# Start addresses of the moving operand in a float32r encoder layer, and another order at its end

## The chip, the cores and the metric

The kernel runs on one core of a Trainium2 chip. The metric is the device time of one execution in microseconds. Three runs of the kernel before took 2140.52, 2140.80 and 2141.89 us; the median is 2140.8 us.

## The reference: what is computed

One inference step of one layer of a streaming encoder, for 256 prompt frames and 32 sample frames (288 together) of width 2048, all in float32:

```
x = x + 1/2 * swiglu(rmsnorm(x, norm_ffn1), w_ffn1_in, w_ffn1_out)      # 2048 -> 2 x 5504 -> 2048
h = rmsnorm(x, norm_mix) @ w_in                                         # columns split among three groups of heads
x = x + concat[GLA 1024 | differential attention 512 | memory attention 512] @ w_o
x = x + 1/2 * swiglu(rmsnorm(x, norm_ffn2), w_ffn2_in, w_ffn2_out)
y = rmsnorm(x, norm_final)
def rmsnorm(x, g): return x * rsqrt(mean(x * x) + 1e-6) * g
def swiglu(x, w_in, w_out):
    gate, up = split(x @ w_in, 2)
    return (silu(gate) * up) @ w_out
```

The memory attention reads 256 memory tokens, which have a projection of their own (`w_mem_kv`). Beside y the step returns keys, values and states.

## The kernel before, in words

**Layout.** The residual `x_res` is kept transposed: the 2048 features lie as 16 blocks of 128 partitions, and each block holds 288 columns, one for each frame. A weight matrix is the stationary operand of a product, in tiles of 128 x 128, and a block of activations of 128 x 288 is the moving operand.

**Split products.** A float32 value is written as the sum of two parts, "high" (rounded to float32r) and "low" (what is left), both of them float32r. Weights are split into `wh` and `wl`, activations into `uh` and `ul` (normed input), `hh` and `hl` (hidden activations), `cdh`/`cdl` and `gch`/`gcl` (outputs of the heads). Three products replace one: wh with high, wh with low, wl with high. `split` (L101) does the first on ScalarE and the second on VectorE.

**Weights.** `add_group` lists all weights in chunks of up to 512 KB in the order of use. `load_chunk` (L163) issues one DMA for each on SP's queue, `split_chunk` (L191) splits it. `consume` (L215) gives the next chunk to the products and on the way brings the splits three chunks ahead and the loads six chunks ahead.

**`gemm` (L271)** makes one output of two blocks of 128 features (`nblk` = 2) in one PSUM tile of two banks. For each chunk of up to four rows of blocks it issues, for block 0 and then block 1, the products of wh with high and low, and then in the same way those of wl with high. Between chunks, `side` gives small steps of other work (attention, transposes, statistics) a place in TensorE's order; each such step is a function in one of four queues (`Thread`), and `need(mark)` runs a queue until a marked step is done.

**Stages.** Memory projection (`mem_group`, products of 512 columns), first feed-forward (`ffn("a", ...)`), input projection of the heads (`MIX`), `w_o` in two halves of eight outputs, second feed-forward (`ffn("b", ..., final=True)`). A feed-forward handles its 43 hidden blocks in two halves of 22 and 21: `gemm` with `w_in` on the normed input, then eight outputs g of `gemm` with `w_out` on the hidden blocks; the second half has 21 rows of blocks in six chunks (4, 4, 4, 4, 4, 1).

**Where the blocks lie.** All blocks of `uh`, `ul`, `hh` and `hl` stand 320 elements (`NS`, 1280 bytes) apart, of which 288 (`NT`) are used, and their tiles begin at 32 modulo 256 bytes of a partition (`uh` at 21024, `ul` at 41504, `hh` at 152096, `hl` at 180256). So every block begins at 32 modulo 256. The operands of `w_o` stand 288 elements (1152 bytes) apart, in tiles that begin at 32 modulo 256 too (`cdh` at 188960, `gch` at 152096), so that blocks begin at 32 and 160 in turn. The tiles of `wh` and `wl`, and each 128-column block in them, begin at 32 modulo 256.

**The end.** After output g of the last half, `final_pair(g)` (L1286) multiplies the two blocks with the final gain into `xg`, adds their squares into `acc` (`prep_sq`) and puts a step on `t_main` that transposes them with TensorE and copies them into the six output tiles `Y`. After g = 6 a step `f7` sums `acc` over the partitions. For g = 7 both blocks get their residual add and their square one after the other; then (L1320 on) TensorE sums the squares for the three groups of frames `T3`, VectorE adds up, `rsq` computes the scale, `need("y7")` transposes the last pair, and the six output tiles are scaled on VectorE and ScalarE in turn and sent by SP.

Of the kernel before, what the change touches and what calls it, by code (L numbers as in the profile page):

```python
# [19 lines left out]
P = 128  # L20
NT = 288
NS = 320
D = 2048
KB = 16
NF = 43
# [15 lines left out]
def hybrid_step_kernel(  # L41
# [40 lines left out]
    def mm(out, lhsT, rhs, start=True, stop=True):  # L82
        pe.matmul(out, lhsT, rhs, start=start, stop=stop)  # L83
# [17 lines left out]
    def split(hi, lo, src):  # L101
        act.copy(hi, src)  # L102
        tt(lo, src, hi.bitcast(F32), ALU.subtract)
# [21 lines left out]
    def kparts(n):  # L125
        return [4] * (n // 4) + ([n % 4] if n % 4 else [])
# [133 lines left out]
    def side(most=2):  # L260
        for t in threads:
            if most and t.can():
                t.step()
                most -= 1
# [3 lines left out]
            t = next(t for t in threads if any(x[1] == mark for x in t.q))  # L268
            t.step()

    def gemm(nchunk, xs, nblk=2):  # L271

        ps = psm.tile([P, 2, 512], F32, tag="m", name=f"m{nxt[2]}")
        k = 0
        for ci in range(nchunk):
            nk, (wh, wl) = consume()
            for part in range(2):
                for b in range(nblk):
                    cs = slice(b * P, (b + 1) * P)
# [12 lines left out]

    fstack = [None]

# [54 lines left out]
    x_res = const.tile([P, KB, NT], F32, name="x_res")  # L349
    G = const.tile([P, G_N], F32, name="G")  # L350
    lam = const.tile([P, 1], F32, name="lam")
    uh = const.tile([P, KB, NS], F32R, name="uh")[:, :, :NT]
    ul = const.tile([P, KB, NS], F32R, name="ul")[:, :, :NT]
    acc = const.tile([P, NT], F32, name="acc")
    dkc = const.tile([P, 4, P], F32, name="dkc")
    dvc = const.tile([P, 512], F32, name="dvc")
# [1 line left out]
    Bs = const.tile([P, 160], F32, name="Bs")  # L358
    mkn = ft.tile([P, P], F32, name="mkn")
    gdk = const.tile([P, 64], F32, name="gdk")  # L360
    mats = const.tile([P, 442], F32, name="mats")
    bcols, tri, smask = mats[:, 0:2], mats[:, 2:130], mats[:, 130:418]

    def gcol(i):
        return G[:, i:i + 1]
# [18 lines left out]

    T3, SR = (0, 128, 160), slice(96, 128)

    def tok_sums(ps, block):

        for t, t0 in enumerate(T3):
            mm(ps[:, t:t + 1], block[:, t0:t0 + P], ones[:, 0:1])  # L390

    fresh = [True]

    def prep_sq(i):
# [9 lines left out]

    def prep_u(i, g0):
        for b in (2 * i, 2 * i + 1):
            gsplit(uh[:, b, :], ul[:, b, :], x_res[:, b, :], gcol(g0 + b))

    def later_R(name):

# [8 lines left out]


    hp = fstack[0][1]
    mTh = hp.tile([P, 22, NS], F32R, tag="hh", name="mTh").rearrange("p a t -> p (a t)")[:, :4096]
    mTl = hp.tile([P, 22, NS], F32R, tag="hl", name="mTl").rearrange("p a t -> p (a t)")[:, :4096]
    mTh = mTh.rearrange("p (k m) -> p k m", m=256)
    mTl = mTl.rearrange("p (k m) -> p k m", m=256)
    mss = sm("mss")
    mrs = sm("mrs")

# [265 lines left out]
    def ffn(tag, mark, g_next, final=False):  # L694
        hp, fp = fstack[0][1], fstack[0][2]

        def ft(nm, bufs):
            return fp.tile([P, 2, NT], F32, tag=nm, bufs=bufs, name=f"{nm}_{tag}")

        def u(k):  # L700
            return uh[:, k, :], ul[:, k, :]

        for half, (a, b) in enumerate(HALVES):
            hh = hp.tile([P, 22, NS], F32R, tag="hh", name=f"hh{tag}{half}")[:, :, :NT]
            hl = hp.tile([P, 22, NS], F32R, tag="hl", name=f"hl{tag}{half}")[:, :, :NT]
            f = a
            while f < b:
                pair = f + 1 < b
                n = 2 if pair else 1
                ps = gemm(4, u)  # L710
                need(mark)
                gs = ft("gs", 1)[:, :n]
                sg = ft("sg", 2)[:, :n]
                mul(gs, ps[:, :n, :NT], Rb(n))
                act.activation(gs, gs, AF.Silu)  # L715
                mul(sg, gs, Rb(n))
                if pair:
                    side()
                    ps = gemm(4, u)
                    up = ps[:, :2, :NT]  # L720
                else:
                    up = ps[:, 1:2, :NT]
                hm = ft("hm", 1)[:, :n]
                mul(hm, up, sg)
                split(hh[:, f - a:f - a + n, :], hl[:, f - a:f - a + n, :], hm)
                f += n
                if f == NF:
                    exp_tables()
                side()
            for g in range(8):  # L730
                ps = gemm(len(kparts(b - a)), lambda k: (hh[:, k, :], hl[:, k, :]))
                xs = x_res[:, 2 * g:2 * g + 2, :]
                if final and half == 1 and g == 7:
                    sq = sq2("sql")
                    last_sq.append(sq)
                    for j in range(2):
                        stt(xs[:, j, :], ps[:, j, :NT], 0.5, xs[:, j, :], ALU.mult, ALU.add)
                        act.activation(sq[:, j, :], xs[:, j, :], AF.Square)
                else:
                    stt(xs, ps[:, :, :NT], 0.5, xs, ALU.mult, ALU.add)  # L740
# [11 lines left out]


    mstack = ExitStack()
    t4p = mstack.enter_context(tc.tile_pool(name="t4p", bufs=8))
    mxp = mstack.enter_context(tc.tile_pool(name="mxp", bufs=1))
    tlp = mstack.enter_context(tc.tile_pool(name="tlp", bufs=2))
# [417 lines left out]
    later_R("mix")  # L1175

    def u(k):
        return uh[:, k, :], ul[:, k, :]

    for kind, c0, g in MIX:  # L1180
        if kind == "glr":
# [98 lines left out]

    later_R("ffn2")
    open_ffn()
    Y = {}
    last_sq = []

    def final_pair(g):  # L1286
        if not Y:
            for t in range(3):
                for hf in range(2):
                    Y[t, hf] = c4(f"y{t}{hf}")  # L1290
        xp = x_res[:, 2 * g:2 * g + 2, :]
        xg = fstack[0][2].tile([P, 2, NT], F32, tag="sg", bufs=2, name="xg")
        for b in range(2):
            ts(xg[:, b, :], xp[:, b, :], gcol(G_FIN + 2 * g + b))
        if g < 7:
            prep_sq(g)
        hf, c0 = divmod(g * 256, 1024)

        def f():
            ps = s1("yt")  # L1300
            for t in range(2):
                for b in range(2):
                    tr(ps[:, t * 256 + b * P:t * 256 + (b + 1) * P], xg[:, b, t * P:(t + 1) * P])
            for t in range(2):
                act.copy(Y[t, hf][:, c0:c0 + 256], ps[:, t * 256:(t + 1) * 256])
# [3 lines left out]
            act.copy(Y[2, hf][96:128, c0:c0 + 256], ps[96:128, :256])  # L1309
        t_main.add(f, f"y{g}", delay=2)  # L1310
        if g == 6:
            def f7():
                ps = s1("yss0")
                tok_sums(ps, acc)
                act.copy(yr[:, 4:7], ps[:, 0:3])
            t_main.add(f7)

    yr = sm("yr")
    ffn("b", "R_ffn2", None, final=True)
    ps = s1("yss")  # L1320
    for j in range(2):
        for t, t0 in enumerate(T3):
            mm(ps[:, 4 * j + t:4 * j + t + 1], last_sq[0][:, j, t0:t0 + P], ones[:, 0:1])
    tt(yr[:, 8:11], ps[:, 0:3], yr[:, 4:7], ALU.add)
    tt(yr[:, 8:11], ps[:, 4:7], yr[:, 8:11], ALU.add)
    rsq(yr[:, 0:3], yr[:, 8:11], float(D))
    need("y7")
    for k, (hf, t, parts) in enumerate(((0, 0, 2), (0, 1, 1), (0, 2, 1), (1, 2, 1), (1, 0, 1), (1, 1, 1))):
        rows = slice(0, P) if t < 2 else slice(96, P)
        dst = y_prompt[0, t * P:(t + 1) * P] if t < 2 else y_sample[0]  # L1330
        n = 1024 // parts
        for c in range(0, 1024, n):
            y = Y[t, hf][rows, c:c + n]
            if k % 2 == 0:
                ts(y, y, yr[rows, t:t + 1])
            else:
                gscale(y, y, yr[rows, t:t + 1])
            sp.dma_start(dst[:, hf * 1024 + c:hf * 1024 + c + n], y)
# [59 lines left out]
```

## Time and profile before

| what | value |
|---|---|
| median of three runs | 2140.8 us |
| the profiled execution | 2142.87 us |
| its span, first to last instruction | 2141.1 us |
| mean granted clock of TensorE | 0.997 |
| TensorE busy | 2125.7 us, 99% |
| VectorE busy | 1116.7 us, 52% |
| ScalarE busy | 867.2 us, 41% |
| DMA: moved, mean rate | 353.75 MB, 165 GB/s |

Busy times of TensorE overlap: the products are pipelined, and each is recorded with its way through the array. A product of 288 columns has about 294 ns in the profile, while the next one starts some 130 ns after it. So what counts for the time is the distance between starts, not the length of one. In the names of a row, "m<-uh,wh" means: a PSUM tile m is written from the moving operand uh and the weights wh.

### The profile page before, as it was taken

To read this page: it belongs to the slowest core of one execution; us is meant where nothing else is said; L and a number is where in the kernel's file an instruction comes from. 1 tells how busy PE (TensorE), PEld (TensorE's weight loads), DVE (VectorE), ACT (ScalarE), POOL (GpSimd) and SP (SyncE) were. 2 spreads that over 40 slices of the span, in tenths; PEclk is the share of its full clock that TensorE was granted. 3 is DMA by queue.
4 is the path that set the end of the run, shared out by engine and by line. 5 is a ranking of instruction groups with operands and counts; after the bars stand their busy time and mean duration, and the time that the engine had idled before them with its cause. 6 is when DMAs were issued, how large, how long until landed. Compare 5 with 4: busy or idle time off the path is not lost.

```text
span 2141.1 us, 37537 instructions
## 1 busy us (share of the span) xinstructions
PE 2125.7 (99%) x16014; PEld 2102.4 (98%) x16014; DVE 1116.7 (52%) x1318; ACT 867.2 (41%) x1112; POOL 4.6 (0%) x11
## 2 busy tenths in 40 slices
PE   9999999999999999999999999999999999999997
PEld 7999999999999999999999999999999999999997
DVE  6754544445454455554665666445544444445443
ACT  6643333333333344334544444333333333333443
POOL 0000000000000000000000000000000000000000
PEclk9999999999999999999999999999999999999999
DMA  7656555555555545555455345555555555555553
GB/s 253 182 178 199 170 169 179 164 164 173 169 159 168 175 158 158 180 144 147 121 157 152 123 158 165 172 167 167 160 170 168 166 165 174 170 167 159 163 160 117
DMA packets 351555, 353.75 MB, mean 165 GB/s; under 512 B 14112, under 2 KB 343324, under 8 KB 351388
## 3 DMA queue, kind: packets, MB, share of 16 engines
q1 hardware_dynamic: 351388, 351.36, 53.9%
q8 instruction: 125, 2.05, 0.4%
q14 instruction: 42, 0.34, 0.0%
HBM read 345.59 MB, written 5.64 MB: 164 GB/s over the span
## 4 chain that ended last, share of the span: by engine, by line
PE 97%; DVE 1%; ACT 1%; DMA 1%; issue 0%; SPq 0%; ACTq 0%; DVEq 0%
PE m L83 93%; DMA ws<-in_w_mem_kv_dram 1%; PE go L83 1%; PE mm L83 0%; DVE wl L90 0%; ACT wh L102 0%; PE mo L83 0%; DVE ul L99 0%; PE gK L83 0%; PE msc L83 0%; PE dsc L83 0%; PE do L83 0%; PE sums L83 0%; DVE acc L90 0%; PE yt L87 0%
## 5 line engine op out<-in xcount | busy, mean ns | idle before, releaser
L90 DVE TENSOR_TENSOR wl<-ws,wh 128x1024 fp32r<-128x1024 f32 (+2 forms) x665 | 781.2, 1189 | 665.9 <-ACT wh L102 636.3
L102 ACT CAST wh<-ws 128x1024 fp32r<-128x1024 f32 (+2 forms) x665 | 665.3, 1018 | 657.9 <-PE m L83 513.9
L83 PE MATMUL m<-uh,wh 128*128 128x288 f32 x3392 | 912.4, 296 | 0.0
L83 PE MATMUL m<-ul,wh 128*128 128x288 f32 x3392 | 907.0, 294 | 0.0
L83 PEld LDWEIGHTS m<-uh,wh 128*128 128x128 f32 x3392 | 637.2, 188 | 2.7 <-issue 1.8
L83 PEld LDWEIGHTS m<-ul,wh 128*128 128x128 f32 x3392 | 637.6, 188 | 0.3
L83 PE MATMUL m<-uh,wl 128*128 128x288 f32 x3392 | 515.5, 294 | 0.0
L83 PEld LDWEIGHTS m<-uh,wl 128*128 128x128 f32 x3392 | 470.6, 188 | 0.0
L83 PE MATMUL m<-hhb,wh 128*128 128x288 f32 x688 | 184.7, 295 | 0.0
L83 PE MATMUL m<-hha,wh 128*128 128x288 f32 x688 | 184.3, 295 | 0.0
L83 PE MATMUL m<-hlb,wh 128*128 128x288 f32 x688 | 184.1, 294 | 0.0
L83 PE MATMUL m<-hla,wh 128*128 128x288 f32 x688 | 184.0, 293 | 0.0
L83 PEld LDWEIGHTS m<-hlb,wh 128*128 128x128 f32 x688 | 129.1, 188 | 0.0
L83 PEld LDWEIGHTS m<-hla,wh 128*128 128x128 f32 x688 | 129.1, 188 | 0.0
L83 PEld LDWEIGHTS m<-hhb,wh 128*128 128x128 f32 x688 | 129.1, 188 | 0.0
L83 PEld LDWEIGHTS m<-hha,wh 128*128 128x128 f32 x688 | 129.0, 188 | 0.0
L83 PE MATMUL m<-hha,wl 128*128 128x288 f32 x688 | 106.3, 294 | 0.0
L83 PE MATMUL m<-hhb,wl 128*128 128x288 f32 x688 | 106.1, 294 | 0.0
L83 PEld LDWEIGHTS m<-hha,wl 128*128 128x128 f32 x688 | 96.0, 188 | 0.0
L83 PEld LDWEIGHTS m<-hhb,wl 128*128 128x128 f32 x688 | 95.9, 188 | 0.0
L715 ACT ACTIVATE gs_b<-gs_b 128x576 f32<-128x576 f32 (+1 forms) x22 | 14.8, 674 | 84.6 <-DVE gs_b L93 84.6
L102 ACT CAST hhb<-hm_b 128x576 fp32r<-128x576 f32 (+1 forms) x22 | 14.6, 662 | 83.2 <-DVE hm_b L93 83.2
(284 smaller groups left out, 1178.0 us busy)
## 6 DMA issues: line engine op xcount, KB each, us to landing
ws<-in_w_ffn_in_dram SPq DMA_DIRECT2D x336, 512.0 KB, 4.1
ws<-in_w_ffn_out_dram SPq DMA_DIRECT2D x160, 512.0 KB, 3.5
ws<-in_w_in_dram SPq DMA_DIRECT2D x80, 512.0 KB, 3.7
ws<-in_w_o_dram SPq DMA_DIRECT2D x32, 512.0 KB, 3.5
ws<-in_w_mem_kv_dram SPq DMA_DIRECT2D x15, 512.0 KB, 5.6
ws<-in_w_ffn_out_dram SPq DMA_DIRECT2D x16, 256.0 KB, 2.7
ws<-in_w_ffn_in_dram SPq DMA_DIRECT2D x16, 256.0 KB, 3.5
x<-in_x_prompt_dram SPq DMA_DIRECT2D x4, 512.0 KB, 7.2
```

What stands on the lines that cost most here:

```text
L83: pe.matmul(out, lhsT, rhs, start=start, stop=stop)
L90: dve.tensor_tensor(out, a, b, op=op)
L102: act.copy(hi, src)
L715: act.activation(gs, gs, AF.Silu)
```

## The change

All blocks of `uh`, `ul`, `hh` and `hl` are moved by 36 elements (`SH`, 144 bytes) inside their tiles, so that they begin at 176 modulo 256 bytes. `uh` and `ul` become one tile `uhl`, which is 8 elements longer than both together; `mats` is 8 elements shorter, so that all tiles behind them keep their place. The tiles of `hh` and `hl` get 64 elements more. The memory projection uses the same tiles, but not the shift. Ahead of the mixer's pools stands a tile of 16 elements (64 bytes), which moves all the mixer's tiles: the operands of `w_o` begin at 96 and 224 modulo 256 bytes in turn.

The last `gemm` (g = 7 of the last half) holds its last two chunks back (`last=2`): after four chunks as before, block 0 gets all its products of the last two (15), and then block 1 gets its own. `final_last` takes the place of what followed: residual add, square and gain for each block, sums of squares added in one PSUM tile `yss` (set to zero by a product with zeros in the step "yss", where the sums of `acc` are added too), transposes and copies for each block apart. The output tiles are scaled and sent in another order: the two of 32 rows come last.

```diff
+SH = 36
...
-    def gemm(nchunk, xs, nblk=2):
+    def gemm(nchunk, xs, nblk=2, last=0):
...
-        for ci in range(nchunk):
+        for ci in range(nchunk - last):
...
+        held = [consume() for _ in range(last)]
+        for b in range(nblk if last else 0):
+            cs = slice(b * P, (b + 1) * P)
+            o, k_ = ps[:, b, :NT], k
+            for i, (nk, (wh, wl)) in enumerate(held):
+                for j in range(nk):
+                    xh, xl = xs(k_ + j)
+                    mm(o, wh[:, j, cs], xh, False, False)
+                    mm(o, wh[:, j, cs], xl, False, False)
+                    mm(o, wl[:, j, cs], xh, False, i == last - 1 and j == nk - 1)
+                k_ += nk
         return ps
+
+    def blocks(pool_, n, name, pad=0, **kw):
+        t = pool_.tile([P, n * NS + pad], F32R, name=name, **kw)
+        return t, lambda k, m=1: (t[:, SH + k * NS:SH + k * NS + NT] if m == 1 else
+                                  t[:, SH + k * NS:SH + (k + m) * NS].rearrange("p (k t) -> p k t", t=NS)[:, :, :NT])
...
-    uh = const.tile([P, KB, NS], F32R, name="uh")[:, :, :NT]
-    ul = const.tile([P, KB, NS], F32R, name="ul")[:, :, :NT]
+    _, uhl = blocks(const, 2 * KB, "uhl", 8)
...
-    mats = const.tile([P, 442], F32, name="mats")
+    mats = const.tile([P, 434], F32, name="mats")
...
-            hh = hp.tile([P, 22, NS], F32R, tag="hh", name=f"hh{tag}{half}")[:, :, :NT]
-            hl = hp.tile([P, 22, NS], F32R, tag="hl", name=f"hl{tag}{half}")[:, :, :NT]
+            hh, hl = (blocks(hp, 22, f"h{c}{tag}{half}", 64, tag=f"h{c}")[1] for c in "hl")
...
+                end = final and half == 1 and g == 7
+                ps = gemm(len(kparts(b - a)), lambda k: (hh(k), hl(k)), last=2 if end else 0)
...
+                if end:
+                    final_last(ps, xs)
+                    continue
...
+    mstack.enter_context(tc.tile_pool(name="pad", bufs=1)).tile([P, 16], F32, name="pad")
...
+    def tok_squares(block, stop):
+        for t, t0 in enumerate(T3):
+            mm(yss[0][:, 0, t:t + 1], block[:, t0:t0 + P], ones[:, 0:1], False, stop and t == 2)
...
             def f7():
-                ps = s1("yss0")
-                tok_sums(ps, acc)
-                act.copy(yr[:, 4:7], ps[:, 0:3])
-            t_main.add(f7)
+                yss.append(s2("yss"))
+                dve.memset(zero3, 0.0)
+                mm(yss[0][:, 0, 0:3], ones, zero3, True, False)
+                tok_squares(acc, False)
+            t_main.add(f7, "yss")
+
+    def final_last(ps, xs):
+        need("yss")
+        xg, sq = gained(7), sq2("sql")
+        pt = []
+        for j in range(2):
+            stt(xs[:, j, :], ps[:, j, :NT], 0.5, xs[:, j, :], ALU.mult, ALU.add)
+            act.activation(sq[:, j, :], xs[:, j, :], AF.Square)
+            ts(xg[:, j, :], xs[:, j, :], gcol(G_FIN + 14 + j))
+        for j in range(2):
+            tok_squares(sq[:, j, :], j == 1)
+            pt.append(s1(f"yl{j}"))
+            if j == 0:
+                for t, t0 in enumerate(T3):
+                    tr(pt[0][:, t * P:(t + 1) * P], xg[:, 0, t0:t0 + P])
+
+        def keep(j):
+            c = 768 + j * P
+            for t in range(2):
+                act.copy(Y[t, 1][:, c:c + P], pt[j][:, t * P:(t + 1) * P])
+            act.copy(Y[2, 1][SR, c:c + P], pt[j][SR, 256:384])
+        for t, t0 in enumerate(T3):
+            tr(pt[1][:, t * P:(t + 1) * P], xg[:, 1, t0:t0 + P])
+        keep(0)
+        rsq(yr, yss[0][:, 0, 0:3], float(D))
+        keep(1)
...
-    for k, (hf, t, parts) in enumerate(((0, 0, 2), (0, 1, 1), (0, 2, 1), (1, 2, 1), (1, 0, 1), (1, 1, 1))):
+    for k, (hf, t, parts) in enumerate(((0, 0, 2), (0, 1, 1), (1, 0, 1), (1, 1, 1), (0, 2, 1), (1, 2, 1))):
```

More of the change, by code (lines that the diff above doesn't have):

```diff
@@ L385, in hybrid_step_kernel @@
     T3, SR = (0, 128, 160), slice(96, 128)
-    def tok_sums(ps, block):
-        for t, t0 in enumerate(T3):
-            mm(ps[:, t:t + 1], block[:, t0:t0 + P], ones[:, 0:1])
     fresh = [True]
@@ L406, in prep_u @@
         for b in (2 * i, 2 * i + 1):
-            gsplit(uh[:, b, :], ul[:, b, :], x_res[:, b, :], gcol(g0 + b))
+            gsplit(uhl(b), uhl(KB + b), x_res[:, b, :], gcol(g0 + b))
     def later_R(name):
@@ L421, in hybrid_step_kernel @@
     hp = fstack[0][1]
[L422 to L425, printed above, removed]
+    mTh, mTl = (blocks(hp, 22, f"mT{c}", 64, tag=f"h{c}")[0][:, :4096].rearrange("p (k m) -> p k m", m=256)
+                for c in "hl")
     mss = sm("mss")
@@ L700, in u @@
         def u(k):
-            return uh[:, k, :], ul[:, k, :]
+            return uhl(k), uhl(KB + k)
         for half, (a, b) in enumerate(HALVES):
-            hh = hp.tile([P, 22, NS], F32R, tag="hh", name=f"hh{tag}{half}")[:, :, :NT]
-            hl = hp.tile([P, 22, NS], F32R, tag="hl", name=f"hl{tag}{half}")[:, :, :NT]
+            hh, hl = (blocks(hp, 22, f"h{c}{tag}{half}", 64, tag=f"h{c}")[1] for c in "hl")
             f = a
@@ L724, in ffn @@
                 mul(hm, up, sg)
-                split(hh[:, f - a:f - a + n, :], hl[:, f - a:f - a + n, :], hm)
+                split(hh(f - a, n), hl(f - a, n), hm if n > 1 else hm[:, 0, :])
                 f += n
@@ L730, in ffn @@
             for g in range(8):
-                ps = gemm(len(kparts(b - a)), lambda k: (hh[:, k, :], hl[:, k, :]))
+                end = final and half == 1 and g == 7
+                ps = gemm(len(kparts(b - a)), lambda k: (hh(k), hl(k)), last=2 if end else 0)
                 xs = x_res[:, 2 * g:2 * g + 2, :]
[L733 to L740, printed above, removed]
+                if end:
+                    final_last(ps, xs)
+                    continue
+                stt(xs, ps[:, :, :NT], 0.5, xs, ALU.mult, ALU.add)
                 if half == 1:
@@ L1177, in u @@
     def u(k):
-        return uh[:, k, :], ul[:, k, :]
+        return uhl(k), uhl(KB + k)
     for kind, c0, g in MIX:
@@ L1282, in hybrid_step_kernel, with gained @@
     open_ffn()
-    Y = {}
-    last_sq = []
+    Y, yss = {}, []
+    def gained(g):
+        return fstack[0][2].tile([P, 2, NT], F32, tag="sg", bufs=2, name="xg")
+    def tok_squares(block, stop):
+        for t, t0 in enumerate(T3):
+            mm(yss[0][:, 0, t:t + 1], block[:, t0:t0 + P], ones[:, 0:1], False, stop and t == 2)
     def final_pair(g):
@@ L1290, in final_pair @@
                     Y[t, hf] = c4(f"y{t}{hf}")
-        xp = x_res[:, 2 * g:2 * g + 2, :]
-        xg = fstack[0][2].tile([P, 2, NT], F32, tag="sg", bufs=2, name="xg")
+        xg = gained(g)
         for b in range(2):
-            ts(xg[:, b, :], xp[:, b, :], gcol(G_FIN + 2 * g + b))
-        if g < 7:
-            prep_sq(g)
+            ts(xg[:, b, :], x_res[:, 2 * g + b, :], gcol(G_FIN + 2 * g + b))
+        prep_sq(g)
         hf, c0 = divmod(g * 256, 1024)
@@ L1312, in f7 @@
             def f7():
-                ps = s1("yss0")
-                tok_sums(ps, acc)
-                act.copy(yr[:, 4:7], ps[:, 0:3])
-            t_main.add(f7)
+                yss.append(s2("yss"))
[27 more added lines that the diff above has]
+        keep(1)
     yr = sm("yr")
+    yr, zero3 = yr[:, 0:3], yr[:, 4:7]
     ffn("b", "R_ffn2", None, final=True)
[L1320 to L1327, printed above, removed]
-    for k, (hf, t, parts) in enumerate(((0, 0, 2), (0, 1, 1), (0, 2, 1), (1, 2, 1), (1, 0, 1), (1, 1, 1))):
-        rows = slice(0, P) if t < 2 else slice(96, P)
+    need("y6")
+    for k, (hf, t, parts) in enumerate(((0, 0, 2), (0, 1, 1), (1, 0, 1), (1, 1, 1), (0, 2, 1), (1, 2, 1))):
+        rows = slice(0, P) if t < 2 else SR
         dst = y_prompt[0, t * P:(t + 1) * P] if t < 2 else y_sample[0]
```

## The prediction

> **What bounds the kernel now.** I read the shares of the span first, then the chain that ended last, then the groups by line, to see which stream of instructions sets the time and how many there are.
>
> ```profile
> PE 2125.7 (99%) x16014; PEld 2102.4 (98%) x16014; DVE 1116.7 (52%) x1318; ACT 867.2 (41%) x1112; POOL 4.6 (0%) x11
> ...
> PE m L83 93%; DMA ws<-in_w_mem_kv_dram 1%; PE go L83 1%; PE mm L83 0%; DVE wl L90 0%; ACT wh L102 0%; PE mo L83 0%; DVE ul L99 0%; PE gK L83 0%; PE msc L83 0%; PE dsc L83 0%; PE do L83 0%; PE sums L83 0%; DVE acc L90 0%; PE yt L87 0%
> ...
> L83 PE MATMUL m<-uh,wh 128*128 128x288 f32 x3392 | 912.4, 296 | 0.0
> L83 PE MATMUL m<-ul,wh 128*128 128x288 f32 x3392 | 907.0, 294 | 0.0
> ...
> L83 PE MATMUL m<-uh,wl 128*128 128x288 f32 x3392 | 515.5, 294 | 0.0
> ...
> L83 PE MATMUL m<-hhb,wh 128*128 128x288 f32 x688 | 184.7, 295 | 0.0
> L83 PE MATMUL m<-hha,wh 128*128 128x288 f32 x688 | 184.3, 295 | 0.0
> ```
>
> TensorE is never short of work: 93% of the chain is the one form "m", a 288-column product, with no idle time before it. VectorE (52%) and ScalarE (41%) follow it. So the time is the number of those products times the distance from one start to the next. The number: three kinds of 3392 on the normed activations (shown), and six of 688 on the hidden activations (two shown; hla and hlb with wh, hha and hhb with wl have the same count): 3 x 3392 + 6 x 688 = 14,304. The w_o stage has six kinds of 128, 768 in all:
>
> ```profile
> L83 PE MATMUL m<-cdh,wh 128*128 128x288 f32 x128 | 35.5, 304 | 0.0
> L83 PE MATMUL m<-cdl,wh 128*128 128x288 f32 x128 | 34.8, 296 | 0.0
> L83 PE MATMUL m<-gcl,wh 128*128 128x288 f32 x128 | 34.6, 294 | 0.0
> L83 PE MATMUL m<-gch,wh 128*128 128x288 f32 x128 | 34.6, 298 | 0.0
> ```
>
> The distance comes from the chain in order of time (start, length, what), in stretches in which it holds nothing but these products; the first row is the memory projection, whose products stream 512 columns:
>
> ```profile
> 16.59 2.76 PE mm L83 x12
> ...
> 290.72 597.24 PE m L83 x4536
> ...
> 1232.32 76.77 PE m L83 x576
> ...
> 1309.57 702.31 PE m L83 x5334
> ...
> 2115.37 0.44 PE yt L87 x4
> ```
>
> 597.24/4536 = 131.67 ns and 702.31/5334 = 131.67 ns: wherever all blocks start at 32 modulo 256, the same figure. In w_o, where starts alternate between 32 and 160, it is 76.77/576 = 133.28 ns. The clock is no part of it; it is granted in full in both stretches (PEclk, third figure):
>
> ```profile
> 290.72:887.96 597.24, 597.24 (x4537) 1.00 0.55 168
> 1232.32:1309.09 76.77, 76.77 (x577) 1.00 0.52 165
> ```
>
> What of 131.67 ns could go? 512 columns take 2.76/12 = 230 ns, so a column costs (230 - 131.67)/(512 - 288) = 0.439 ns, 288 of them 126.4, and 5.3 ns are paid per product whatever its length. Why w_o pays more is seen in the start times, first there, then in a feed-forward stage, and last the weight loads of the latter:
>
> ```profile
> 1292.97 0.29 PE L83 MATMUL m<-gch,wh 128*128 128x288 f32 x1
> 1293.10 0.29 PE L83 MATMUL m<-gcl,wh 128*128 128x288 f32 x1
> 1293.23 0.30 PE L83 MATMUL m<-gch,wh 128*128 128x288 f32 x1
> 1293.37 0.29 PE L83 MATMUL m<-gcl,wh 128*128 128x288 f32 x1
> 1293.50 0.29 PE L83 MATMUL m<-gch,wh 128*128 128x288 f32 x1
> ```
>
> ```profile
> 1600.13 0.29 PE L83 MATMUL m<-hhb,wh 128*128 128x288 f32 x1
> 1600.26 0.29 PE L83 MATMUL m<-hlb,wh 128*128 128x288 f32 x1
> 1600.39 0.30 PE L83 MATMUL m<-hhb,wh 128*128 128x288 f32 x1
> 1600.53 0.29 PE L83 MATMUL m<-hlb,wh 128*128 128x288 f32 x1
> ...
> 1600.13 0.19 PEld L83 LDWEIGHTS m<-hlb,wh 128*128 128x128 f32 x1
> ```
>
> Both streams step by 0.13, 0.13 and 0.14 us: a common step with a longer one now and then. In w_o the long step is the one between the two products of a block that starts at 160 (1293.23 to 1293.37); a block at 32 after it, or before it, costs no more than usual. And each weight load begins with the product before it (both rows at 1600.13), so two reads run at once, now both from starts at 32 modulo 256. The phase of a block thus is a lever of some ns per product; which phase is best no row tells.
>
> **The change, part by part.** First, **the uniform blocks**: 14,304 products go from 32 to 176; no instruction is added. The new distance D is in no row, so bounds. Gain side: the whole 5.3 ns goes, D = 126.4, 14,304 x 5.3 ns = 75.8 us. Loss side, the nearest phase: if the 32s in w_o keep 131.67, its 160s cost 2 x 133.28 - 131.67 = 134.89 ns; 160 is 16 bytes from 176, and 3.22 ns x 14,304 = 46.1 us. Which row is 176 nearest to? By bytes the 160, by kind the feed-forward row: after the change these blocks still all share one phase, and w_o's surcharge stands in one step of four where two phases meet, so I don't charge it. I take half of the 5.3 ns as gone, since the row of 32 is where both reads start in step, and a shift of 144 bytes takes them apart: D = 129.0, 14,304 x 2.65 ns = 37.9 us gained. This is a choice between bounds, not a reading.
>
> The Trainium skill ("TensorE: Matmul & The Clock Gate", Part 2, step 1) says that the moving operand and the weight load have SBUF read ports of their own, so that loading the next weights takes nothing from the running matmul. By that rule phases would not matter and this term would be 0; 133.28 beside 131.67 ns speaks against it. Its formula for a warm matmul (Back-to-back issue gap: columns over 2.4 GHz plus 2.5 ns) would give an estimate of 122.5 ns and a gain of up to 131 us.
>
> Second, **w_o**: 768 products, from 32 and 160 to 96 and 224. Two phases still meet. Bounds: 133.28 - 126.4 = 6.9 ns off (5.3 us), or the same surcharge once more, 3.2 ns on (2.5 us). I take 0.
>
> Third, **the end**, the timeline from the last product on, which starts at 2126.67:
>
> ```profile
> 2127.00 0.82 DVE L99 SCALAR_TENSOR_TENSOR x_res<-m,x_res 128x288 f32<-128x288 f32 x2 [9.23 <-PE m L83]
> 2127.49 0.81 ACT L738 ACTIVATE sql<-x_res 128x288 f32<-128x288 f32 x2 [7.55 <-DVE x_res L99]
> ...
> 2127.99 1.50 PE L83 MATMUL yss<-ones,sql 128*128 128x1 f32 x12 [1.02 <-ACT sql L738]
> ...
> 2129.60 0.35 DVE L90 TENSOR_TENSOR yr<-yss,yr 128x3 f32<-128x3 f32 x2 [1.22 <-PE yss L83]
> 2129.99 0.17 DVE L371 TENSOR_SCALAR rs<-yr 128x3 f32<-128x3 f32 x1
> ...
> 2130.53 0.63 ACT L1305 COPY y<-yt 128x256 f32<-128x256 f32 x2
> ...
> 2131.19 0.36 ACT L1309 COPY y<-yts 32x256 f32<-32x256 f32 x1
> 2131.25 2.45 DVE L96 TENSOR_SCALAR y<-y,yr 128x512 f32<-128x512 f32 x4
> 2131.58 3.49 ACT L106 ACTIVATE y<-y,yr 128x1024 f32<-128x1024 f32 x3
> 2131.76 4.19 SPq L1338 DMA_DIRECT2D out_dram<-y  x7
> ...
> SPq L1393 <- DMA out_dram<-y: 4.1, 4, 1.3
> ...
> out_dram<-y SPq DMA_DIRECT2D x2, 128.0 KB, 3.8
> ```
>
> (The last two rows: what SP waits for at the very end, in us, times and longest; and the two 32-row output transfers with their size and time to landing.)
>
> The last two of the six chunks (5 of 21 rows of blocks) are held back, so block 0 gets its 15 products, then block 1 its 15 (15 x 131.67 ns = 1.98 us). Under those lie block 0's residual add (0.41), square (0.41) and gain; if the add waits for the whole PSUM tile instead of its half, that cover is gone. After block 1: its add and square (0.82), beside which TensorE sums block 0's squares (half of 1.50); then three transposes of block 0 (0.44/4 = 0.11 each by the yt row of the chain above) and the other half of the sums. The two adds on VectorE (0.35) are replaced by accumulation in PSUM. So the scale's computation starts near 2127.0 + 0.82 + 0.33 + 0.75 = 2128.9, not at 2129.99: 1.1 us. Block 0's copies go into ScalarE's queue ahead of the logarithm; they are there before it is needed. The copies of 0.63 and 0.36 us, partly after the exponential, are split over both sides: some 0.3 us. In the output, the two 128-row halves (1, 0) and (1, 1) move ahead of the two 32-row ones; all seven DMAs stay in SP's queue, which has nothing else left, and the last one to go is now 128 KB, not 512. Added on the path: a zero matmul in the step "yss" inside the last product group (0.13 us by the yss rows: 1.50/12), whose memset is long done on an idle VectorE. Bounds 0 to 3.5 us gained (nothing if the cover is gone and the transfers set the end; 2 us more than I take if half of the 4.1 us in which SP waits for landings drops out); I take 1.5, the 1.1 + 0.3 and 0.1 for the rest.
>
> Sum: 37.9 + 0 + 1.5 = 39.4 us. The profiled execution took 2142.87 us, 1.77 around its span of 2141.1, and lies 2.07 above the median of 2140.8. 2142.87 - 39.4 = 2103.5 in the profile's terms, 2101.4 in the median's.
>
> **The rivals.** *All of it goes*: D = 126.4 everywhere, 75.8 + 5.3 + 1.5 = 82.6 us, 2058.2. For it: 5.3 ns is overhead; against it: in no row is any of it missing.
>
> *The phase does nothing here*: the surcharge belongs to mixed phases alone, or the weight load sets the step, and uniform blocks cost 131.67 ns at any one phase. Only the end moves: 2140.8 - 1.5 = 2139.3. For it: three separate kinds of block, two stages, one figure; against it: the long step stands between two products of the same phase. The Trainium skill ("SBUF — State Buffer", Specifications) has lines of 16 bytes, with a penalty per line; 32, 160, 176, 96 and 224 are all multiples of 16, so this rule too would change nothing, and 133.28 ns disagrees with it.
>
> *176 behaves like 160* (the other side): its place is every one of the 14,304 products, its price 3.22 ns each, 46.1 - 1.5 = 44.6 us more, 2185.4. It decides from 0.41 ns per product on ((4.3 + 1.5)/14,304). For it: 16 bytes' distance, and the long step lies within a 160 block; if every step there were long by 8 to 10 ns it would be worse still. Against it: averaged over four steps w_o loses only 1.6 ns.
>
> **How the numbers follow.** A run of this kernel tells a difference from about 0.2% (4.3 us) on. Chances: the forecast 0.60 (own range 2068 to 2136, that is 5.0 to 0.2 ns gone per product), all of it 0.09, nothing 0.09, like 160 0.22. Faster 0.60 + 0.09 = 0.69, same 0.09, slower 0.22. The range goes from 2062, which leaves out most of the second case, to 2180, which leaves out about half of the fourth.
>
> **What would show it.** In the chain of waits, a long stretch of "PE m" in the feed-forward divided by its count: 129.0 for the forecast, 126.4, 131.67 or 134.9 for the others; in w_o near 133.3. The granted clock must stay 1.00. At the end, the first operation of the scale about 1.9 us after the last product, and a span that ends some 12.6 us after it, not 14.1. Wrong I am if the feed-forward figure rises, or if VectorE or ScalarE, with their writes at new phases, hold TensorE back: idle time before "m" would then be other than 0.0.

## The result, and the profile after

The changed kernel takes 2128.93 us (median of six runs, 2128.58 to 2129.34) beside 2142.07 us for the kernel before in the same comparison (six runs, 2140.52 to 2142.39). The ratio is 0.994 [0.993, 0.995]: 13.1 us faster, where 39.4 were forecast.

The shares of the span, the largest group by line and the last product's surroundings of the kernel after; the next fence is its chain of waits in order of time (start, length, what), with the same stretches as before:

```profile
PE 2111.5 (99%) x16016; PEld 2088.4 (98%) x16016; DVE 1116.6 (52%) x1317; ACT 868.0 (41%) x1114; POOL 4.6 (0%) x11
...
L84 PE MATMUL m<-uhl,wh 128*128 128x288 f32 x6784 | 961.9, 294 | 0.0
```

```profile
66.74 34.33 PE m L84 x264
...
287.63 594.72 PE m L84 x4536
...
1223.01 76.41 PE m L84 x576
...
1299.90 699.35 PE m L84 x5334
...
2016.95 16.38 PE m L84 x126
2033.99 16.52 PE m L84 x126
```

TensorE still bounds the kernel, with no idle time before its main group; VectorE's and ScalarE's busy times are where they were. What has changed is the distance between starts, and it has two values: 594.72/4536 = 131.11 ns and 699.35/5334 = 131.11 ns in the two long stretches, but 16.38/126 = 130.00 ns and 16.52/126 = 131.11 ns side by side in stretches of one and the same stage, at the same addresses. Before, every stretch of uniform blocks had 131.67 ns. Over all 14,304 products the start times give means of 130.85 ns (normed input), 131.11 (first feed-forward, hidden) and 130.79 (second), 130.88 together: 14,304 x 0.78 = 11.2 us. In w_o it is 76.41/576 = 132.66 instead of 133.28 ns: 768 x 0.62 = 0.5 us.

The end, in the timeline of the kernel after (start, length, engine, line, operation, and in brackets the idle time before it and its releaser), with what SP waits for at the very end:

```profile
2113.17 0.29 PE L84 MATMUL m<-hhb,wl 128*128 128x288 f32 x1
2113.49 0.46 DVE L100 SCALAR_TENSOR_TENSOR x_res<-m,x_res 128x288 f32<-128x288 f32 x1 [9.32 <-PE m L84]
2113.99 0.44 ACT L1340 ACTIVATE sql<-x_res 128x288 f32<-128x288 f32 x1 [10.28 <-DVE x_res L100]
...
2114.27 0.45 DVE L100 SCALAR_TENSOR_TENSOR x_res<-m,x_res 128x288 f32<-128x288 f32 x1
...
2116.30 0.16 DVE L389 TENSOR_SCALAR rs<-yss 128x3 f32<-128x3 f32 x1 [1.17 <-PE yss L84]
...
2117.56 2.33 DVE L97 TENSOR_SCALAR y<-y,yr 128x512 f32<-128x512 f32 x4
...
2118.07 5.46 SPq L1374 DMA_DIRECT2D out_dram<-y  x7
...
SPq L1429 <- DMA out_dram<-y: 2.3, 4, 1.0
```

The last product starts at 2113.17. Both residual adds stand behind it: block 0's, which was to lie under block 1's 15 products, starts at 2113.49 after 9.32 us of idle time. The add waits for the PSUM tile with both banks, not for its half. The scale starts 2.83 us after the end of the last product (2116.30 - 2113.47; "end" is the start plus 0.29 or 0.30 us), before it was 3.0 (2129.99 - 2126.98), and the span ends 13.4 us after it, before 14.1.

So the last product ends 13.5 us earlier (2126.98 to 2113.47), and what follows is 0.7 us shorter. Of the 13.5 us, 0.7 come from the start of the first such product (66.74, before 67.45), behind the first loads, 11.2 and 0.5 from the distances; some 1.1 us lie in pieces between the stretches that I didn't trace further. The profiled execution before was 0.8 us above its median, so part of these 1.8 us is no property of the change.

### The profile page after: what moved, and what is told of

The parts are those of the page before. It is cut to its first block, busy times and chain, and to the rows that moved or that the text cites. A ratio compares the mean times of both kernels' runs of the same rounds, so it can differ in the third digit from the quotient of the medians.

```text
span 2126.9 us, 37539 instructions
## 1 busy us (share of the span) xinstructions
PE 2111.5 (99%) x16016; PEld 2088.4 (98%) x16016; DVE 1116.6 (52%) x1317; ACT 868.0 (41%) x1114; POOL 4.6 (0%) x11
## 4 chain that ended last, share of the span: by engine, by line
PE 96%; ACT 1%; DMA 1%; DVE 1%; issue 0%; SPq 0%; ACTq 0%
PE m L84 93%; DMA ws<-in_w_mem_kv_dram 1%; PE go L84 1%; ACT wh L103 0%; DVE wl L91 0%; ACT uhl L107 0%; PE mo L84 0%; PE gK L84 0%; PE msc L84 0%; PE dsc L84 0%; PE do L84 0%; PE sums L84 0%; ACT x_res L472 0%; PE yt L88 0%; ACT sq L410 0%
## 5 line engine op out<-in xcount | busy, mean ns | idle before, releaser
L84 PE MATMUL m<-uhl,wh 128*128 128x288 f32 x6784 | 961.9, 294 | 0.0
L84 PEld LDWEIGHTS m<-uhl,wh 128*128 128x128 f32 x6784 | 911.8, 188 | 3.1 <-issue 1.8
L84 PE MATMUL m<-uhl,wl 128*128 128x288 f32 x3392 | 512.5, 293 | 0.0
L84 PEld LDWEIGHTS m<-uhl,wl 128*128 128x128 f32 x3392 | 468.2, 188 | 0.0
L103 ACT CAST hha<-hm_a 128x576 fp32r<-128x576 f32 (+1 forms) x22 | 14.6, 663 | 81.3 <-DVE hm_a L94 81.3
L725 ACT ACTIVATE gs_a<-gs_a 128x576 f32<-128x576 f32 (+1 forms) x22 | 14.8, 674 | 79.1 <-DVE gs_a L94 79.1
```

## The experiments

The theory after the result: the distance (moving block's start minus weight tile's start, modulo 256 bytes) sets a repeating pattern of steps, and 176 with weights at 32 gives a pattern that can repeat in two ways. Rivals: the start of the moving block by itself counts; the end, not the addresses, made the gain; 176 happens to be near some smooth optimum. In the kernels below the starts of the blocks are set apart for each stage: `SH` elements of 4 bytes, so that a block begins at 32 + 4 SH modulo 256. "u" is the normed input of the first feed-forward, the heads' projection (mix) and the second feed-forward, "h" the hidden blocks of the two halves of each feed-forward. Distances between starts are from the first and last start of the longest stretch; the windows (start and end, length, TensorE's busy time and number of products, granted clock, DMA share, GB/s) agree to about 0.15 ns, and those of 14 and 17 us to about 0.5 ns, if 0.29 us is added to the length, since products that began before the window are counted too. A rate "in part" is that of other stretches of the same stage.

**e1_end_alone: the new end without the new addresses.**

```diff
-SH = 36
+SH = 0
...
-    mstack.enter_context(tc.tile_pool(name="pad", bufs=1)).tile([P, 16], F32, name="pad")
```

> The kernel after with all blocks back at 32 modulo 256 bytes and those of w_o back at 32 and 160 (SH = 0, no tile ahead of the mixer's pools); the new end stays. If the phases make nearly all of the gain of 13 us, this is 0.5 to 1.5 us faster than the kernel before (the span after the last product went from 14.1 to 13.4 us), its feed-forward stretches are back at 131.67 ns per product and w_o at 133.3. If the gain came from the end or from anything else that the new layout brings (one tile for both parts of the normed input), it is 10 us or more faster and the stretches stay below 131.67.

2140.47 us (11 runs) beside 2141.42 (15 runs), ratio 0.9998 [0.9989, 1.0007]. Its chain of waits:

```profile
1230.31 76.77 PE m L84 x576
...
1307.57 702.31 PE m L84 x5334
```

131.67 and 133.28 ns are back. The span ends 13.4 us after the last product here too, so the trace has the end's 0.7 us; as a time it can't be told from nothing. The gain is the addresses'.

**e2_wo_back: w_o's operands back at 32 and 160, everything else as after.**

```diff
-    mstack.enter_context(tc.tile_pool(name="pad", bufs=1)).tile([P, 16], F32, name="pad")
```

> The kernel after without the 64-byte tile ahead of the mixer's pools, so that only the operands of w_o go back to 32 and 160. If the w_o stage has a rate of its own, set by its own phases, it goes from 132.66 back to 133.3 ns, 768 x 0.6 ns = 0.5 us slower than the kernel after, and all other stretches keep 130.0 or 131.1 ns. If the rates of the feed-forward hang on more than the phase of their own blocks (what came before them), some of them change although their blocks did not move.

2129.91 us (4 runs), ratio 0.9947 [0.9934, 0.9961]. The chain of waits:

```profile
1222.57 76.73 PE m L84 x576
...
1299.79 699.35 PE m L84 x5334
```

w_o alone goes back, to 76.73/576 = 133.21 ns; the uniform blocks keep 131.11. The tile ahead of the mixer's pools is worth about 0.5 us by the trace (768 x 0.6 ns), too little to show in the time.

**scan1 and scan2: other starts for the blocks, weights at 32.** All else is as after. The first diff is scan1, the second scan2; `SHU` goes by the first gain index of the stage (16 first feed-forward, 33 mix, 49 second feed-forward), `SHH` by feed-forward and half.

```diff
-SH = 36
+SHU = {16: 32, 33: 16, 49: 24}
+SHH = {"a0": 56, "a1": 8, "b0": 48, "b1": 40}
```

```diff
-SH = 36
+SHU = {16: 4, 33: 20, 49: 52}
+SHH = {"a0": 60, "a1": 12, "b0": 44, "b1": 28}
```

> The kernel after with another start in each stage (modulo 256 bytes): first feed-forward input 160, its hidden halves 0 and 64, mixer input 96, second feed-forward input 128, its hidden halves 224 and 192. If 160 is bad by itself (the rival that 176 behaves like 160), the first feed-forward's input products run at 134.9 ns or, if each step is long, near 139; if the long step in w_o came from two phases meeting, 160 alone runs below 133. If half of the 5.3 ns can be had at some phase, one of these stages runs at 129.0 or less; if the fixed part cannot go, all lie between 130 and 135.

> As the first scan, with first feed-forward input 48, its hidden halves 16 and 80, mixer input 112, second feed-forward input 240, its hidden halves 208 and 144. Both together show 14 of the 16 starts that are multiples of 16 bytes. If the rate follows the distance to 160 or to 32, neighbours have neighbouring rates and 144 is like 160 and 176; if it follows the place in 64 bytes, 48, 112, 176 and 240 have one rate, 130.0 to 131.1. A start below 130.0 ns would show that the forecast's 129.0 was there to be had at another place.

Their times for one run each, 2155.21 and 2149.24 us, mix seven starts and aren't used. Windows of scan1 (160, 0, 128, 224), then of scan2 (48, 112, 240, 208):

```profile
500.00:750.00 250.00, 250.00 (x1878) 1.00 0.55 165
360.00:480.00 120.00, 120.00 (x903) 1.00 0.51 164
1330.00:1580.00 250.00, 250.00 (x1901) 1.00 0.56 167
1600.00:1720.00 120.00, 120.00 (x902) 1.00 0.52 166
```

```profile
495.00:740.00 245.00, 245.00 (x1863) 1.00 0.57 168
1118.00:1135.00 17.00, 17.00 (x132) 1.00 0.61 176
1320.00:1570.00 250.00, 250.00 (x1877) 1.00 0.56 166
1592.00:1715.00 123.00, 123.00 (x938) 1.00 0.53 169
```

With 32 (before) and 176 (after) that gives all multiples of 16, weights at 32:

| start | distance to weights | ns from start to start | | start | distance | ns |
|---|---|---|---|---|---|---|
| 32 | 0 | 131.67 | | 160 | 128 | 133.33 |
| 48 | 16 | 131.67 (130.00 in part) | | 176 | 144 | 130.00 or 131.11 |
| 64 | 32 | 133.33 | | 192 | 160 | 133.33 |
| 80 | 48 | 132.50 | | 208 | 176 | 131.43 |
| 96 | 64 | 131.67 (132.22 in part) | | 224 | 192 | 133.33 |
| 112 | 80 | 131.11 | | 240 | 208 | 133.33 |
| 128 | 96 | 131.67 | | 0 | 224 | 133.33 |
| 144 | 112 | 134.53 (133.26 in part) | | 16 | 240 | 131.99 |

The clock is 1.00 in every row, and TensorE is busy throughout. The figures are not smooth: 176 has the lowest, but its neighbours 160 and 192 the common 133.33 and 144 the highest. Nothing is below 130.00, so 126.4 and 129.0 ns are reached by no start that is a multiple of 16. The sensitivity of 3.2 ns that the rival "176 behaves like 160" assumed is there (130.00 to 133.33), only its sign at 176 isn't.

**weights_192: all weight tiles 160 bytes on, from 32 to 192.** If distance counts, the list above moves with the weights; if the block's start counts, it stays.

```diff
-SH = 36
+SHU = {16: 40, 33: 12, 49: 24}
+SHH = {"a0": 48, "a1": 60, "b0": 20, "b1": 8}
...
+    pool("padx").tile([P, 28], F32, name="padx")
...
-    _, uhl = blocks(const, 2 * KB, "uhl", 8)
+    _, uhl = blocks(const, 2 * KB, "uhl", 60)
...
-    mats = const.tile([P, 434], F32, name="mats")
+    mats = const.tile([P, 418], F32, name="mats")
```

(The hidden blocks' tiles begin at 64 here, so that these stand at 0, 48, 144 and 96.)

> The weight tiles moved from 32 to 192 modulo 256 bytes (by 160), and the moving blocks at first feed-forward input 192, its hidden halves 0 and 48, mixer input 80, second feed-forward input 128, its hidden halves 144 and 96. If the distance between the two reads counts, the rates are those that the scans showed 160 bytes lower: 131.67 (as 32), 131.67 (as 96), 134.5 or 133.3 (as 144), 131.1 or 130.0 (as 176), 133.33 (as 224), 133.33 (as 240), 133.33 (as 192). If the moving block's own address counts, they are those of the scans at the same place: 133.33, 133.33, 131.67 or 130.0, 132.5, 131.67, 134.5 or 133.3, 131.67. If both count in another way, neither list comes.

2152.85 us in one run. Windows of starts 192, 48, 80 and 128:

```profile
495.00:745.00 250.00, 250.00 (x1901) 1.00 0.55 165
760.00:870.00 110.00, 110.00 (x819) 1.00 0.54 170
893.00:920.00 27.00, 27.00 (x210) 1.00 0.63 180
1325.00:1575.00 250.00, 250.00 (x1878) 1.00 0.55 167
```

| start | distance | by distance | by the start | measured, ns |
|---|---|---|---|---|
| 192 | 0 | 131.67 | 133.33 | 131.67 |
| 0 | 64 | 131.67 or 132.22 | 133.33 | 132.22 |
| 48 | 112 | 134.53 or 133.26 | 131.67 or 130.00 | 134.67 |
| 80 | 144 | 130.00 or 131.11 | 132.50 | 130.00 and 131.10 |
| 128 | 192 | 133.33 | 131.67 | 133.33 |
| 144 | 208 | 133.33 | 134.53 or 133.26 | 133.33 |
| 96 | 160 | 133.33 | 131.67 or 132.22 | 133.30 |

All seven follow the distance to within 0.15 ns; the list by start misses six of them by 1 ns or more and fits only 144, by its second figure. So the two starts, the moving block's and the weight tile's, set the step together. The Trainium skill ("TensorE: Matmul & The Clock Gate", Part 2, step 1) has separate read ports by which the weight load takes nothing from a running product; by that the table would show one figure, and the runs show up to 4.7 ns between them. Why the distance counts no run shows.

**scan3: starts that are not multiples of 16.**

```diff
-SH = 36
+SHU = {16: 34, 33: 37, 49: 22}
+SHH = {"a0": 38, "a1": 35, "b0": 18, "b1": 46}
```

> Starts that are no multiples of 16 bytes: first feed-forward input 168, its hidden halves 184 and 172, mixer input 180, second feed-forward input 120, its hidden halves 104 and 216 (weights at 32). If lines of 16 bytes are what a read pays for, these starts touch 73 lines, not 72, and all run slower than their neighbours, near 133.33 ns. If the rate is a smooth function of the start, 168 to 184 run at 130.0 to 133.3 around 176, and 104 and 120 between 131.1 and 131.7. If rates lock in steps of a beat of 6.67 ns (20 beats a product, and one beat less in every second, third, fourth ...), each rate is 133.33 less 6.67/n: 130.0, 131.11, 131.67, 132.0 or 133.33.

2178.5 us in one run. Windows of 168, 184, 180 and 120:

```profile
505.00:760.00 255.00, 255.00 (x1877) 1.00 0.54 161
365.00:485.00 120.00, 120.00 (x902) 1.00 0.51 165
1145.00:1162.00 17.00, 17.00 (x128) 1.00 0.60 176
1345.00:1600.00 255.00, 255.00 (x1915) 1.00 0.55 166
```

136.00 (168), 133.33 (184), 133.33 (172), 134.69 (180), 133.34 (120), 133.33 (104) and 133.32 (216): none is below 133.3, and of the four starts tried around 176 none is better. The rates of 136.00 and 134.69 lie above 133.33, which the forecast with beats did not allow. The Trainium skill ("SBUF — State Buffer", Specifications) lets one expect a loss, with lines of 16 bytes and a penalty for each new line. The four starts around 176 cost 2 to 6 ns more than 176, but that is no proof of the rule: five of the seven starts run at 133.3 ns, as six multiples of 16 do, and 184 costs no more than its neighbour 192.

**columns: what a column costs.** The hidden products stream 280, 272, 256 and 224 columns in the four halves, except the first product of each sum. The outputs of the columns left out lack most of their sum; the streams and instructions stay.

```diff
+                ps = gemm(len(kparts(b - a)), lambda k: (hh(k), hl(k)), last=2 if end else 0,
+                          nt={"a0": 280, "a1": 272, "b0": 256, "b1": 224}[f"{tag}{half}"])
```

> The kernel after, in which the products on the hidden activations (all but the first one of each sum) stream fewer columns: 280 and 272 in the two halves of the first feed-forward, 256 and 224 in those of the second; what the missing columns should add is left out. By the prediction's line (0.439 ns a column, and a fixed part) from 131.1 ns: 127.6, 124.1, 117.1 and 103.0. If a product takes its columns in beats of 16 (6.67 ns) and two beats more, less one in every second or third product: near 127.8, 123.3 to 124.4, 116.7 to 117.8 and 103.3 to 104.4. If the weight load sets the step, it does not fall below some floor, and the shorter ones stay at 120 or more.

2085.35 us in one run. Windows of the four halves, first here, then of the kernel after with 288 columns:

```profile
350.00:475.00 125.00, 125.00 (x964) 1.00 0.53 172
750.00:865.00 115.00, 115.00 (x925) 1.00 0.57 178
1570.00:1680.00 110.00, 110.00 (x936) 1.00 0.59 191
1955.00:1969.00 14.00, 14.00 (x127) 1.00 0.56 181
```

```profile
350.00:475.00 125.00, 125.00 (x956) 1.00 0.53 171
...
1570.00:1680.00 110.00, 110.00 (x841) 1.00 0.51 166
```

129.89, 124.55, 117.84 and 112.06 ns (112.6 in the six shorter stretches with 224 columns), beside 131.11. The prediction's line and the beats both come within 0.8 ns at 272 and 256 columns, and both miss by 2 ns or more at 280 and by 7 ns or more at 224; a floor of 120 ns isn't there. Between 288 and 256 columns a column costs (131.11 - 117.84)/32 = 0.415 ns, which leaves 131.11 - 288 x 0.415 = 11.6 ns per product; but 8 columns cost 1.22 ns from 288 to 280 and 5.34 from 280 to 272, and 32 columns only 5.78 from 256 to 224. The step does not grow evenly with the columns, so the prediction's 5.3 ns, the difference of two lengths drawn out over 288 columns, had no firm value: a line through other lengths gives twice as much. Its 230 ns had none either: eleven steps of 512 columns on end average 227.6 to 231.4 ns in different places of the memory projection before, which by the same division leaves 8.3 to 3.5 ns per product.

The Trainium skill ("TensorE: Matmul & The Clock Gate", Back-to-back issue gap) has columns over 2.4 GHz plus 2.5 ns for a matmul by itself, and says that in a stream with weight loads both set the spacing, which the prediction's 122.5 ns left out. What the runs have above columns over 2.4 GHz is 11.1, 13.2, 11.2, 11.2 and 18.7 ns for 288, 280, 272, 256 and 224, so its 2.5 ns is not reached in these streams.

**restart1: is the pattern chosen where a stretch begins?** In the kernel after, some short stretches reach 130.00, the long ones stay at 131.11. One product of another kind (a transposition whose output nobody reads) interrupts TensorE's stream once in each feed-forward, after 10 pairs in the first and 1 pair in the second.

```diff
             while f < b:
...
+                if half == 0 and f == (20 if tag == "a" else 2):
+                    tr(s1("again")[:, :P], ident)
```

> The kernel after with one transposition of the identity matrix into a spare PSUM tile, twice in the program: in the first feed-forward after its tenth pair of hidden blocks, in the second after its first pair. If the same addresses have two locked rates (130.00 and 131.11 ns), and where a stretch starts decides between them, the stretches behind the transpositions (some 4,500 and 5,100 products) may come out at 130.00: 5 us or 10 us faster than the kernel after, or the same within 0.5 us if the dice fall as before. If 131.11 in the long stretches comes from the traffic that runs there (loads, splits), a restart changes nothing.

2118.87 us (4 runs, 2118.17 to 2119.75), ratio 0.9895 [0.9878, 0.9911]. The chain of waits around the first restart, and the long stretch behind the second:

```profile
318.80 0.11 PE again L88
318.91 558.49 PE m L84 x4296
...
1317.07 671.59 PE m L84 x5166
```

558.49/4296 = 130.00 ns and 671.59/5166 = 130.00 ns. Two idle transpositions make the kernel 10 us faster than the change alone: 4296 + 5166 products x 1.11 ns = 10.5 us. No address differs. The run columns shows both rates without a transposition: of the normed-input products of its second feed-forward, whose addresses and lengths are those of after, the 2087 that begin at 1290.9 us run at 131.11 ns and the 2016 that begin at 1689.0 us, behind shortened products, at 130.00.

**restart_32: the same restarts with the blocks at 32** (`SH = 0`, all else as restart1).

```diff
-SH = 36
+SH = 0
```

> The two transpositions of the first restart in the kernel after with the blocks of uh, ul, hh and hl back at 32 modulo 256 bytes; w_o at 96 and 224 and the new end stay. If a second locked rate exists only at some distances between the moving block and the weights (144, and not 0, where every stretch so far ran at 131.67 ns), this stays at 131.67 everywhere and within 2 us of the kernel before. If a restart helps wherever it stands, the stretches behind it fall below 131.67 and it gains 5 us or more.

2141.34 us (10 runs), ratio 0.9998 [0.9989, 1.0008]. The chain of waits:

```profile
321.58 565.64 PE m L84 x4296
...
1330.60 680.19 PE m L84 x5166
```

565.64/4296 = 131.67 ns and 680.19/5166 = 131.67 ns. At distance 0 no second rate shows, here or in before and e1_end_alone; the restart does nothing by itself.

**restart2: two transpositions in a row.**

```diff
+                if half == 0 and f == (20 if tag == "a" else 2):
+                    z = s1("again")
+                    for q in range(2):
+                        tr(z[:, q * P:(q + 1) * P], ident)
```

> The restart with two transpositions in a row in place of one, blocks at 176. If the entry into a stretch decides the lock as dice do, each of the two long stretches comes out at 130.00 or 131.11 ns with about even chances: 2118.9, 2124 or 2129 us. If the transposition itself changes something for good (a rate of 130.00 after any of them), both come out at 130.00 and the time is 2119 again.

Four runs: 2124.66, 2119.14, 2120.90 and 2118.74 us; ratio 0.9897 [0.9880, 0.9913]. The profiled one is the first; its chain of waits:

```profile
319.58 558.48 PE m L84 x4296
...
1317.93 677.32 PE m L84 x5166
```

The first long stretch has 130.00 ns, the second 677.32/5166 = 131.11: 5.7 us more, and this run lies 5.9 us above the fastest. So one program falls into either rate. The other three executions have no trace; by their times both stretches would be at 130.00, or nearly. It isn't all chance: the six stretches of 126 products in the last half run at 130.00, 130.00, 131.11, 130.00, 130.00 and 131.11 ns in after, e2_wo_back, restart1 and restart2 alike. What decides is open.

**low_apart: high parts at 176, low parts elsewhere.** Products of high and low alternate, so this asks whether two starts in turn do better than one.

```diff
-SH = 36
+SHL = {16: 4, 33: 20, 49: 16, "a0": 0, "a1": 24, "b0": 44, "b1": 52}
+SHU = {16: 36, 33: 36, 49: 36}
+SHH = {"a0": 36, "a1": 36, "b0": 36, "b1": 36}
```

> The high parts at 176 as in the kernel after, the low parts elsewhere: first feed-forward input 48, its hidden halves 32 and 128, mixer input 112, second feed-forward input 96, its hidden halves 208 and 240. If each product's cost is that of its own distance, the means lie at a third of the low part's rate and two thirds of 130.0 to 131.1: 130.6 to 131.9 ns. If two starts that take turns can take the beat from more products than every second one, some stage runs below 130.0, and the forecast's 129.0 is within reach; if taking turns only costs, as in w_o, they lie above the thirds.

2140.71 us in one run. Windows of low parts at 32, 128 and 48:

```profile
355.00:480.00 125.00, 125.00 (x964) 1.00 0.53 171
760.00:870.00 110.00, 110.00 (x848) 1.00 0.54 174
500.00:740.00 240.00, 240.00 (x1818) 1.00 0.56 167
```

Low parts at 32 and at 128 give 130.00 ns over the whole of their half, though either start alone has 131.67; 240 gives 130.24, 96 131.67, 208 131.93, 48 132.21, 112 132.5. So a mixture is not one third of the low part's rate and two thirds of 176's: 32, 128 and 240 lie below that, 96, 208, 48 and 112 above. No mixture is below 130.00.

**low_128: high parts at 176, low parts at 128 in all stages, no restart.**

```diff
-SH = 36
+SH, SL = 36, 24
...
-            gsplit(uhl(b), uhl(KB + b), x_res[:, b, :], gcol(g0 + b))
+            gsplit(uhl(b, sh=SH), uhl(KB + b, sh=SL), x_res[:, b, :], gcol(g0 + b))
```

> The kernel after with the low parts of all uniform blocks at 128 and the high parts left at 176, no restart; w_o and the end as they are. In the run with low parts apart, the hidden products with the low part at 128 ran at 130.00 ns in a stretch of 1006. If that pair of starts has one locked rate, all uniform stretches run at 130.00 whatever comes before them: 14,304 x (130.88 - 130.00) ns = 12.6 us faster than the kernel after, about 2116, with little spread. If it has two rates like 176 alone, some stretches come out near 131.1 and the time lies between 2117 and 2129.

2116.39 us (4 runs, 2116.32 to 2116.72), ratio 0.9882 [0.9866, 0.9899] beside 2141.76: the fastest of all, 12.5 us under the changed kernel's median, with the runs 0.4 us apart. Its chain of waits:

```profile
287.02 589.69 PE m L84 x4536
...
1293.62 693.44 PE m L84 x5334
```

589.69/4536 = 130.00 ns and 693.44/5334 = 130.00 ns, with nothing to restart the stream. (131.67 - 130.05) x 14,304 = 23.2 us of the 25.4 are the uniform products; 130.05 is the mean over all of them.

## Why the prediction was wrong in size

**The direction held, and of the mechanism that the two reads meet.** The prediction read from w_o's start times that the phase of a moving block costs or saves some ns per product, and from the rows at 1600.13 that a weight load runs beside the product before it, so that two reads meet. e1 (no gain without the addresses) and weights_192 (the distance between the two reads, seven of seven) bear out both. The 2128.9 us lie inside the range, far from 2101.4. The reason given for the gain did not hold: "the row of 32 is where both reads start in step, and a shift of 144 bytes takes them apart". Starting in step (distance 0) has 131.67 ns; of the other fifteen distances nine are dearer, three the same in their main rate and three cheaper. That 144 bytes is one of the three was luck, since no row of before told it.

**The step that failed is D = 129.0**, "I take half of the 5.3 ns as gone". It measured 130.88: 0.78 ns gone instead of 2.65, 11.2 us instead of 37.9, which is nearly the whole miss. The prediction called it a choice between bounds. Two more things in it were wrong. The 5.3 ns itself came from two lengths, and the columns run shows no even price per column. And the gain was thought of as a share that a shift takes away smoothly, while the mean rates mostly take a few values, 133.33, 131.67, 131.11 and 130.00 in the tables, with none under 130.00. Even the best that distance 144 showed, 131.67 - 130.00 = 1.67 ns, would have been 23.9 us over 14,304 products; half of that was not had, because the long stretches ran at 131.11. The prediction's reading of its rows, a common step with a longer one now and then, was right. In the trace's start times, which are to the nanosecond, one step of four is longer both in the feed-forward before (130, 131, 130, 135 ns) and in w_o (132, 132, 130, 139); in after the stretches at 130.00 have 129 and 131 ns in turn, and the long ones 130, 132 and 131. So the shift changed the pattern of the steps, and no row of before told the size of a new one.

**w_o, taken as 0, measured -0.6 ns**, 0.5 us, within its bounds.

**The end, taken as -1.5 us, measured -0.7.** The prediction named the case: "if the add waits for the whole PSUM tile instead of its half, that cover is gone". It does, so both adds stand behind the last product, and the scale starts 2.83 us after it instead of the forecast 1.9 (0.17 us gained, not 1.1). The rest comes at the output: SP waits 2.3 us for landings instead of 4.1, but its seven DMAs are issued over 5.46 us instead of 4.19.

**The rivals.** "All of it goes" (126.4) is refuted by every scan. "The phase does nothing here" is refuted by after and weights_192; its other half, that the end alone moves the time by little, is right (e1). "176 behaves like 160" is refuted: 160 has 133.33 ns alone, 176 at most 131.11. But the prediction's ground for not charging it was wrong: it had w_o's surcharge "where two phases meet", while its own rows put the long step between two products of one block, and 160 alone costs 133.33 (scan1). The rival was not far-fetched: of the sixteen starts six are at 133.33 and three more above 131.67 (134.53, 132.50 and 131.99); a move of 16 bytes to either side, or any start off 16 bytes that was tried, would have made the kernel slower than before. VectorE and ScalarE, whose writes moved too, hold nothing back: the idle time before "m" is still 0.0.

## What to carry to other kernels

When back-to-back products set the time, divide the long stretches of the chain by their count and compare stages: a difference of 1 ns in 130 is 0.8% of the kernel, and the start of the moving block against the weight tile, modulo 256 bytes, is worth trying at every multiple of 16, since neighbours tell nothing of each other. Look at short and long stretches apart: if one stage shows two rates at the same addresses, a mean hides it, and an interruption or a second start taken in turn can bring the better one. Don't split a per-product overhead from two lengths and then spend a share of it; say the smallest and largest rate that some row shows, and stay near them.

## What the runs showed of the hardware that was not expected

- The step between products depends on the distance of the two reads modulo 256 bytes, from 130.00 to 134.67 ns at 288 columns for starts that are multiples of 16 bytes, up to 136.00 at others, and not evenly.
- Several mean rates fit one arithmetic: 133.33 ns less 6.67 ns once in n products gives 130.00 (n = 2), 131.11 (3), 131.67 (4), 132.00 (5), 132.22 (6) and 132.50 (8). This is a fit to means only: 131.43, 134.53, 134.69 and 136.00 are not among them, and single steps don't follow it, since a stretch at 130.00 has steps of 129 and 131 ns. Whether there is such a beat no run shows.
- At distance 144 a stream keeps one of two rates, 130.00 or 131.11, for thousands of products, and one unrelated product between two of them can change it (restart1); two in a row did so in one place and not in the other, in the profiled execution (restart2). Distances 16, 64 and 112 show two rates as well (the table of the scans). What decides is open.
- High parts at 176 and low parts at 128 in turn held 130.00 ns in all long stretches, though a stream at 128 alone has 131.67. Why is open too. For w_o's operands, whose blocks stand 1152 bytes apart, a distance of 144 throughout was not tried.
